# One layer of a two-layer DiT block: ctx's feed-forward network in a pass of its own, lat's up projection by seven products

## The chip, the cores and the metric

The kernel runs on one core of a Trainium2 chip. The metric is device time in microseconds: the median of three runs is 3036.41 us (3034.74 to 3040.76). Besides these there is one execution under the hardware profiler, and every row below is from it.

## The reference, cut to what matters

Two token streams go through two layers: lat, 1024 tokens, and ctx, 256 tokens, both of width 1024, all in float32. In layer 1 ctx only feeds lat's mixers; its own output is not needed there, so its feed-forward network (FFN) runs in layer 0 alone.

```python
def conv_ffn(h, w_up, conv_w, conv_b, w_down):
    u = dwconv(h @ w_up, conv_w, FFN_CONV // 2) + conv_b      # w_up 1024 x 5632, 3 taps along the tokens
    gate, val = jnp.split(u, 2, axis=-1)                      # D_FF = 2816 columns each
    return (jax.nn.silu(gate) * val) @ w_down                 # 2816 x 1024

for layer in range(DEPTH):                                    # DEPTH = 2
    mod = sc @ ada_w[layer] + ada_b[layer]                    # conditioning: 6 x 1024 numbers per stream
    mod_c = scc @ ada_w[layer] + ada_b[layer]
    ...
    y_l, y_c = token_mixer(h_l, h_c, w_in[layer], w_out[layer], ...)
    x = x + g1[:, None, :] * y_l
    x = x + g2[:, None, :] * conv_ffn(modulate(x, norm_ffn_g[layer], sh2, sc2), ffn_w_up[layer], ...)
    if want_ctx:                                              # layer 0 only
        h_ctx = h_ctx + g1c * y_c
        h_ctx = h_ctx + g2c * conv_ffn(modulate(h_ctx, norm_ffn_g[layer], sh2c, sc2c), ffn_w_up[layer], ...)
return rmsnorm(x, final_norm_g)
```

## The kernel before, in words

Activations lie transposed: 128 channels on the partitions, tokens along the free axis, so lat is 8 tiles of 128x1024 and ctx 8 tiles of 128x256. A float32 product is made of three passes of TensorE over operands cut in two parts: ACT casts the raw tile to the high part (L315), DVE subtracts it to get the low part (L316), and the passes are high by high, high by low, low by high (`mm3`, L341). A weight of 1024x128 is loaded as 512 KB into a raw tile (`load_w`, L325). The raw tiles come from rings "wr" and "wd" of one buffer each, the cut parts from rings "wh" and "wl" of two each. So a raw tile is loaded again only when its subtraction is done. PSUM holds two tiles of 1024 columns ("a") and four of 512 ("b").

A scheduler writes one queue per engine in advance. An engine works off its queue in that order; DMAs are issued by SP (weights) and POOL (activations), in order as well.

Each layer has these stages: the mixers (projections of lat and ctx, a gated scan, window attention, a linear recurrence); `project_out` (L1145 ff), in two parts of 512 lat tokens; the norm; the up projection; the down projection `lat_down`. The stages that the change touches are:

- **Layer 0's FFN** (`ffn_up`, about 790 to 1491 us of the span). For each of 22 column tiles f and for gate and value it loads one 512 KB tile of W_up. With that it makes 48 products of 512 columns for lat (tile `pu`) and 24 of 256 columns for ctx (`puc`). The convolution is one ACT operation and two on DVE (L1277 to L1279). For every two f, ctx's down products (`pd`, 48 of 256 columns) are made and added to the residual `xc` on DVE (L1257). A row block of W_down (`dr`, 512 KB) is loaded and cut for that, on ACT and DVE.
- **Layer 1's up projection** (`ffn_up7`, 2317 to 2783 us) has lat only. It cuts the 2x2 block product into seven products of sums of blocks (Strassen's scheme), tiles `ux` and `uz` (L1445): for each f 7 x 12 = 84 products of 512 columns for gate and value together, where the plain form has 96. The sums of activations are made in `sums7` (L1473) after the norm `norm7`, the sums of weights on DVE, beside the products.
- **Lat's down projection** (`lat_down`, tiles `px` and `py`, L1661): seven stages of six operand pairs each, in both layers. Its activations come back from DRAM (`park`); in layer 0 those of even f stay partly in SBUF.
- **The conditioning** (`ada_gen`): one step loads 512 KB of ada_w (`aw`, L190) and makes 4 float32 products of 256 columns (`ada`, L199; 8 records in the trace). A generator has 16 such steps. Those of layer 1's second and third part (32 steps) lie in layer 0: 28 in its FFN, 4 in its attention.
- **The final norm** (`fin`, L1681 to L1692): eight rows of 128 tokens, each transposed on TensorE, squared on ACT, scaled on DVE and stored. The last four come after the last product.

The rows name two more operations: L916, in attention, is the only elementwise work on POOL; L1409 and L1410 are the convolution in layer 1.

Of the kernel before, what the change touches and what calls it, by code (L numbers as in the profile page):

```python
# [18 lines left out]
P = 128  # L19
# [68 lines left out]
def tile_dit(ctx: ExitStack, tc: tile.TileContext, x, c, ctxt, c_ctx, ada_w, ada_b, norm_mix_g, norm_ffn_g,  # L88
# [371 lines left out]
    def ada_tile():  # L460
        aring[1] += 1
        return wtile(aring[0][aring[1] % len(aring[0])], "aw", F32, 1)

    adas += [ada_gen(l_, t_, ada_tile) for l_, t_ in ((0, 1), (0, 2), (1, 0), (1, 1), (1, 2))]
# [85 lines left out]
    def mixers(l, hl, hc, steps):  # L550
# [339 lines left out]

        lrus = [lru(p) for p in range(2)]
# [173 lines left out]
        def att_step(s_):  # L1065
# [17 lines left out]
            if l == 0 and s_ % 2 and s_ < 4 * len(grp) - 40:  # L1083
                ada_step()
# [38 lines left out]
        if l == 0:  # L1123
            ada_fin(0, 1)
# [19 lines left out]
    def project_out(l, y, xl, xc):  # L1144
# [18 lines left out]
        for part in range(2):  # L1163
            for m in range(KT):
# [28 lines left out]
    def ffn_up(l, h, hc_, xc, bt, pre_):  # L1193


        WU, WD = ffn_w_up[l], ffn_w_down[l]
        u_, odd, even, grp, cq = {}, {}, [], [], []
        jobs = [(0, h, T), (1, hc_, C)]

        def up_w(f, val):  # L1200
            return load_w((ALL, ALL, ALL, w_cols(WU, (f + NF * val) * P)))

        pre = {(0, v): up_w(0, v) for v in range(2)}
        yield "ready"

        def b_tile(a, j):
            if PAIRS[j][1] == 2:
                bt[a, 0, j] = two(L("b"))
            else:
                bt["odd", a] = two(L("b"))  # L1210
                bt[a, 0, j] = bt["odd", a][:, 0:1, :]

        def lat_act(f, g, u):
            fh, k = f % 2, f // 2
            j, i = k // 2, k % 2
            if fh == 0:
                if i == 0:
                    b_tile(fh, j)
                for b, o in ((0, bt[fh, 0, j][:, i, :]), (1, u[:, 512:1024])):
                    V.tensor_tensor(out=o, in0=g[:, b * 512:b * 512 + 512], in1=u[:, b * 512:b * 512 + 512], op=mult)  # L1220
            else:
                V.tensor_tensor(out=u, in0=g, in1=u, op=mult)
                G.dma_start(out=park[l][1, 0, j][:, i, :], in_=u[:, 0:512])
            if fh == 0:
                even.append(u)
                return
            e = even.pop()
            G.dma_start(out=park[l][1, 1, j][:, i, :], in_=u[:, 512:1024])
            V.tensor_tensor(out=e[:, 512:1024], in0=u[:, 512:1024], in1=e[:, 512:1024], op=sub)
            G.dma_start(out=park[l][0, 1, j][:, i, :], in_=e[:, 512:1024])  # L1230

        def ctx_act(f, a):

# [3 lines left out]
            split(dh, dl, dr)  # L1237
            ac = H2("ac", F32R)
            ah, al = ac[:, 0:C], ac[:, C:2 * C]
            split(ah, al, a)  # L1240
            grp.append((dh, dl, ah, al))
            if f % 2:
                g_ = list(grp)
                grp.clear()
                cq.extend((g_, m) for m in range(0, KT, 2))

        def ctx_down(g_, m):
            pd = pb1("pd")
            for i, (dh, dl, ah, al) in enumerate(g_):
                for m_ in range(2):  # L1250
                    c_ = slice((m + m_) * P, (m + m_ + 1) * P)
                    for pi in range(3):
                        PE.matmul(out=pd[:, m_ * C:(m_ + 1) * C], lhsT=(dl if pi == 2 else dh)[:, c_],
                                  rhs=al if pi == 1 else ah, start=(i == 0 and m_ == 0 and pi == 0),
                                  stop=(i == 1 and pi == 2), skip_group_check=True)
            for m_ in range(2):
                V.scalar_tensor_tensor(out=xc[m + m_], in0=pd[:, m_ * C:(m_ + 1) * C], scalar=mod[l][:, 40 + m + m_, 1:2],  # L1257
                                       in1=xc[m + m_], op0=mult, op1=add)

        def up(f, val):  # L1260
            col = f + NF * val
            wh, wl = pre.pop((f, val)) if (f, val) in pre else up_w(f, val)

            def cw(j):
                return rows[f"fcw{l}{j}"][:, col:col + 1]

            ada_load()
            if (f, val) == (NF - 1, 1):
                pre_()
            for s_, hh, n in jobs:  # L1270
                pu = pb1("puc")[:, 0:C] if s_ else ps("pu")
                for b in ((BC,) if s_ else (B0, B1)):
                    mm3(pu[:, b], wh, wl, *cut(hh, b))
                u = H2("uc")[:, 0:C] if s_ else L("u")
                if not val:
                    u_[s_, f] = u
                S.activation(out=u, in_=pu, func=AF.Identity, scale=cw(1), bias=rows[f"fcb{l}"][:, col:col + 1])  # L1277
# [10 lines left out]
            if not val:  # L1288
                while cq:
                    ctx_down(*cq.pop(0))  # L1290
            ada_mm()

        for f in range(NF):
            up(f, 0)
            up(f, 1)
# [512 lines left out]
```

## Time and profile before

| what | value |
|---|---|
| median of three runs | 3036.41 us |
| the profiled execution, its own time | 3035.6 us |
| its span, first to last instruction | 3033.8 us |
| TensorE busy | 2877.1 us, 95% |
| VectorE (DVE) busy | 1902.6 us, 63% |
| ScalarE (ACT) busy | 1420.8 us, 47% |
| GpSimd (POOL) busy | 236.5 us, 8% |
| mean granted TensorE clock | 0.981 |
| moved by DMA | 335.75 MB, mean 111 GB/s |

The span is 1.8 us shorter than the execution's own time. Busy time of TensorE is counted as the union of its pipelined products; the number of products in a stretch says more than the busy share where the clock falls. Stages have different limits, so the shares of the whole span say little about a single stage.

### The profile page before, as it was taken

To read this page: it belongs to the slowest core of one execution; us is meant where nothing else is said; L and a number is where in the kernel's file an instruction comes from. 1 tells how busy PE (TensorE), PEld (TensorE's weight loads), DVE (VectorE), ACT (ScalarE), POOL (GpSimd) and SP (SyncE) were. 2 spreads that over 40 slices of the span, in tenths; PEclk is the share of its full clock that TensorE was granted. 3 is DMA by queue.
4 is the path that set the end of the run, shared out by engine and by line. 5 is a ranking of instruction groups with operands and counts; after the bars stand their busy time and mean duration, and the time that the engine had idled before them with its cause. 6 is when DMAs were issued, how large, how long until landed. Compare 5 with 4: busy or idle time off the path is not lost. (4 is left out here: it accounts for less than half of the span.)

```text
span 3033.8 us, 41821 instructions
## 1 busy us (share of the span) xinstructions
PE 2877.1 (95%) x16208; PEld 2273.7 (75%) x16208; DVE 1902.6 (63%) x3005; ACT 1420.8 (47%) x2445; POOL 236.5 (8%) x348
## 2 busy tenths in 40 slices
PE   6999898999999999999999899998998899999998
PEld 5867676558888888888878787676667688877776
DVE  5466555665644444444587756776757777776876
ACT  5366764663422222222334545784745555544333
POOL 2000002000000000000101000002010011112010
PEclk9999999999999999999999999999999899999999
DMA  7211246424322332222576200124043333336762
GB/s 296 70 60 53 66 128 187 121 90 126 98 91 95 101 101 77 77 66 74 186 253 186 94 29 22 36 63 108 11 162 99 77 98 94 95 94 205 261 190 90
DMA packets 286678, 335.75 MB, mean 111 GB/s; under 512 B 19180, under 2 KB 211856, under 8 KB 286480
## 3 DMA queue, kind: packets, MB, share of 16 engines
q1 hardware_dynamic: 242928, 231.29, 24.6%
q0 software_dynamic: 43376, 101.73, 11.2%
q8 instruction: 128, 2.10, 0.3%
q14 instruction: 70, 0.57, 0.1%
q10 hardware_dynamic: 176, 0.07, 0.0%
HBM read 276.65 MB, written 56.36 MB: 110 GB/s over the span
## 5 line engine op out<-in xcount | busy, mean ns | idle before, releaser
L1445 PE MATMUL ux<-t,sw 128*128 128x512 f32 x1320 | 319.9, 398 | 20.5 <-ACT t L315 10.8
L1445 PEld LDWEIGHTS ux<-t,sw 128*128 128x128 f32 x1320 | 248.2, 190 | 85.3 <-ACT t L315 13.4
L341 PE MATMUL pu<-hh,wh 128*128 128x512 f32 x704 | 278.9, 397 | 0.1
L341 PE MATMUL pu<-hh,wl 128*128 128x512 f32 x704 | 276.5, 393 | 0.0
L341 PE MATMUL pu<-hl,wh 128*128 128x512 f32 x704 | 275.4, 391 | 0.0
L1278 DVE SCALAR_TENSOR_TENSOR u<-pu,col_fcb,u 128x1023 f32<-128x1023 f32 x44 | 56.4, 1283 | 324.6 <-ACT u L1277 324.6
L315 ACT CAST wh<-wr 128x1024 fp32r<-128x1024 f32 x110 | 115.2, 1049 | 230.8 <-PE pc L341 66.6
L341 PE MATMUL pl<-hh,wh 128*128 128x512 f32 x512 | 211.3, 413 | 2.0 <-ACT wh L315 0.8
L341 PE MATMUL pl<-hh,wl 128*128 128x512 f32 x512 | 205.7, 402 | 1.1 <-DVE wl L316 1.1
L341 PE MATMUL pl<-hl,wh 128*128 128x512 f32 x512 | 205.4, 401 | 0.0
L1277 ACT ACTIVATE u<-pu,col_nf,col_fcw 128x1024 f32<-128x1024 f32 x44 | 53.0, 1206 | 318.9 <-PE pu L341 318.9
L316 DVE TENSOR_TENSOR wl<-wr,wh 128x1024 fp32r<-128x1024 f32 x110 | 136.0, 1236 | 69.4 <-ACT wh L315 62.3
L341 PEld LDWEIGHTS pu<-hh,wh 128*128 128x128 f32 x704 | 132.3, 188 | 38.8 <-issue 11.8
L315 ACT CAST ah<-raw 128x512 fp32r<-128x512 f32 x132 | 76.0, 618 | 182.0 <-PE px L1661 89.3
L341 PEld LDWEIGHTS pu<-hh,wl 128*128 128x128 f32 x704 | 132.3, 188 | 29.1 <-DVE uc L1278 0.6
L341 PEld LDWEIGHTS pu<-hl,wh 128*128 128x128 f32 x704 | 132.4, 188 | 28.0 <-issue 0.2
L1445 PE MATMUL uz<-t,sw 128*128 128x512 f32 x528 | 132.4, 398 | 0.7 <-DVE cv L1460 0.7
L341 PEld LDWEIGHTS pl<-hh,wh 128*128 128x128 f32 x512 | 96.4, 188 | 35.2 <-issue 14.0
L1445 PEld LDWEIGHTS uz<-t,sw 128*128 128x128 f32 x528 | 100.5, 191 | 24.4 <-DVE cv L1460 1.6
L1011 DVE TENSOR_REDUCE st<-sc 128x1 f32<-128x641 f32 (+2 forms) x144 | 106.8, 745 | 17.8 <-ACT sc L1010 16.2
L341 PEld LDWEIGHTS pl<-hh,wl 128*128 128x128 f32 x512 | 96.6, 189 | 26.4 <-issue 5.1
L1014 ACT ACTIVATE pb<-sc,st 128x641 f32<-128x641 f32 (+2 forms) x144 | 106.3, 739 | 20.4 <-DVE st L1011 17.4
(464 smaller groups left out, 7352.6 us busy)
## 6 DMA issues: line engine op xcount, KB each, us to landing
raw<-in_ffn_w_down_dram SPq DMA_DIRECT2D x220, 256.0 KB
aw<-in_ada_w_dram SPq DMA_DIRECT2D x96, 512.0 KB
wr<-in_ffn_w_up_dram SPq DMA_DIRECT2D x44, 512.0 KB
b<-act POOLq DMA_DIRECT2D x35, 512.0 KB, 8.9
wr<-in_w_in_dram SPq DMA_DIRECT2D x34, 512.0 KB
act<-u POOLq DMA_DIRECT2D x66, 256.0 KB, 3.6
wr<-in_w_out_dram SPq DMA_DIRECT2D x128, 128.0 KB
dr<-in_ffn_w_down_dram SPq DMA_DIRECT2D x22, 512.0 KB
```

What stands on the lines that cost most here:

```text
L315: S.copy(out=hi, in_=raw)
L316: eng.tensor_tensor(out=lo, in0=raw, in1=hi.bitcast(F32), op=sub)
L341: PE.matmul(out=o, lhsT=wl[k] if pi == 2 else wh[k], rhs=hl[k] if pi == 1 else hh[k], start=(k == 0 and pi == 0), stop=(k == nk - 1 and pi ...
L1011: V.tensor_reduce(out=st[:, 0, c_], in_=sc[:, s0:769], axis=mybir.AxisListType.X, op=ALU.min)
L1014: S.activation(out=pb, in_=sc[:, s0:769], func=AF.Exp, bias=st[:, 0, c_], scale=-1.0, accum_out=st[:, 1, c_])
L1277: S.activation(out=u, in_=pu, func=AF.Identity, scale=cw(1), bias=rows[f"fcb{l}"][:, col:col + 1])
L1278: V.scalar_tensor_tensor(out=u[:, 1:n], in0=pu[:, 0:n - 1], scalar=cw(0), in1=u[:, 1:n], op0=mult, op1=add)
L1445: PE.matmul(out=out, lhsT=(al if pi == 2 else ah)[:, k * P:(k + 1) * P], rhs=rhs[k][1 if pi == 1 else 0], start=(i in (1, 2, 7) and k == 0 ...
```

## The change

In layer 0, `ffn_up` goes. In its place stand `ffn_ctx`, a pass over the 22 column tiles for ctx alone, and then `ffn_up7` for lat, as in layer 1. W_up of layer 0 is therefore loaded twice. In `ffn_ctx`, gate's raw weight uses the ring "wr" and value's the ring "wd"; the low part of the down weight is made on POOL; all 8 x 256 columns of ctx's output are summed over all f in the two large PSUM tiles and added to the residual once, at the end. Lat's norm of the upper half of the tokens and the sums of `sums7` are steps that are dealt out over the pass, two to a column tile at first, then one. `project_out` makes ctx's part in its first part instead of the second, and ctx's norm lies in the second part.

The 32 conditioning steps are now taken in layer 1's projections and attention, where their weight tile is again on the rings. Layer 0's norm steps at the end of `lat_down` are grouped. The last four rows of the final norm are cut: transposing, squaring and scaling by the weight for channels 512 to 1023 is done within the last stage, and only channels 0 to 511 come after it, with one reciprocal root for the four rows.

```diff
-    adas += [ada_gen(l_, t_, ada_tile) for l_, t_ in ((0, 1), (0, 2), (1, 0), (1, 1), (1, 2))]
+    adas += [ada_gen(l_, t_, ada_tile) for l_, t_ in ((0, 1), (0, 2), (1, 0))]
...
+        if l:
+            adas.extend(ada_gen(1, t_, ada_tile) for t_ in (1, 2))
...
-            if l == 0 and s_ % 2 and s_ < 4 * len(grp) - 40:
+            if s_ % 2 and s_ < 4 * len(grp) - (1 - l) * 40:
                 ada_step()
...
-                if part == 1 and xc is not None:
+                if part == 0 and xc is not None:
...
-    def ffn_up(l, h, hc_, xc, bt, pre_):
+    def ffn_ctx(l, hc_, xc):
...
+        po = [ps("pd") for _ in range(2)]
+        pd = [po[m // 4][:, m % 4 * C:(m % 4 + 1) * C] for m in range(KT)]
...
+            return load_w((ALL, ALL, ALL, w_cols(WU, (f + NF * val) * P)), ring=("wr", "wd")[val])
...
             dr = L("dr")
             nc.sync.dma_start(out=dr, in_=WD[f * P:(f + 1) * P, :])
             dh, dl = L("dh", F32R), L("dl", F32R)
-            split(dh, dl, dr)
+            split(dh, dl, dr, G)
+            return dh, dl
...
+        for f in range(NF):
+            ada_load()
+            u_ = []
+            for val in range(2):
+                col = f + NF * val
+                wh, wl = up_w(f, val)
+                if val == 0:
+                    dw = down_w(f)
...
+                pu = pb1("puc")[:, 0:C]
+                mm3(pu, wh, wl, *cut(hc_, BC))
...
+            if due:
+                down(*due.pop())
+            V.tensor_tensor(out=u_[0], in0=u_[0], in1=u_[1], op=mult)
             ac = H2("ac", F32R)
             ah, al = ac[:, 0:C], ac[:, C:2 * C]
+            split(ah, al, u_[0])
+            due.append((f, *dw, ah, al))
+            ada_mm()
+            yield
+        down(*due.pop())
+        for m in range(KT):
+            V.scalar_tensor_tensor(out=xc[m], in0=pd[m], scalar=mod[l][:, 40 + m, 1:2], in1=xc[m], op0=mult, op1=add)
...
+        fa, up_ = [lambda r=r: fin(r, xa) for r in range(4)], [lambda i=i: upper(i) for i in range(4)]
+        return [all_of(*fa[0:2]), all_of(*fa[2:4], up_[0]), all_of(*up_[1:4])], lower
...
-        f_ = ffn_up(l, h2, h2c, xc, bt, lambda: next(d_)) if want else ffn_up7(l, xl, tb, lambda: next(d_))
-        next(f_)
-        run(steps0)
+        f_ = ffn_up7(l, xl, tb, lambda: next(d_))
+        n1 = norm7(xl, 1, l, xmid[l], tb)
         if want:
...
+            run(stepsc)
+            todo, n1 = steps0 + n1[0:1], n1[1:]
+            todo += sums7(xl, tb, n1)
+            aring[0] = None
+            for i_, _ in enumerate(ffn_ctx(l, h2c, xc)):
+                run(todo, 1 + (i_ < 6))
+                if i_ == NF - 1:
+                    next(f_)
+            aring[0] = ["wd"]
+            next(f_)
+            run(todo)
```

Two places show what moves. The first is SP's queue at the start of layer 0's FFN. Before, `wr_7283` and `wr_7289` are gate and value of f = 0, `wr_7630` and `wr_7726` those of f = 1, then f = 2; `aw` is conditioning; `dr_7617` and `dr_7822` are the down weights of f = 0 and f = 1.

```order
L325 DMA wr_7283<-in_ffn_w_up_dram 128x8x128
L190 DMA aw_7439<-in_ada_w_dram 128x1024
L325 DMA wr_7289<-in_ffn_w_up_dram 128x8x128
L325 DMA wr_7630<-in_ffn_w_up_dram 128x8x128
L190 DMA aw_7529<-in_ada_w_dram 128x1024
L190 DMA aw_7636<-in_ada_w_dram 128x1024
L190 DMA aw_7732<-in_ada_w_dram 128x1024
L1235 DMA dr_7617<-in_ffn_w_down_dram 128x1024
L325 DMA wr_7726<-in_ffn_w_up_dram 128x8x128
L325 DMA wr_7835<-in_ffn_w_up_dram 128x8x128
L325 DMA wr_7991<-in_ffn_w_up_dram 128x8x128
L1235 DMA dr_7822<-in_ffn_w_down_dram 128x1024
```

The same place on SP in the changed kernel, from the down weight of f = 0 on. `wr_7405` and `wr_7447` are gate and value of f = 1, `wr_7524` and `wr_7566` of f = 2, `wr_7667` and `wr_7709` of f = 3, `wr_7780` and `wr_7822` of f = 4; `dr_7411`, `dr_7530` and `dr_7673` are the down weights of f = 1, 2 and 3.

```order
L1207 DMA dr_7316<-in_ffn_w_down_dram 128x1024
L325 DMA wr_7405<-in_ffn_w_up_dram 128x8x128
L325 DMA wr_7447<-in_ffn_w_up_dram 128x8x128
L325 DMA wr_7524<-in_ffn_w_up_dram 128x8x128
L325 DMA wr_7566<-in_ffn_w_up_dram 128x8x128
L325 DMA wr_7667<-in_ffn_w_up_dram 128x8x128
L325 DMA wr_7709<-in_ffn_w_up_dram 128x8x128
L1207 DMA dr_7411<-in_ffn_w_down_dram 128x1024
L325 DMA wr_7780<-in_ffn_w_up_dram 128x8x128
L325 DMA wr_7822<-in_ffn_w_up_dram 128x8x128
L1207 DMA dr_7530<-in_ffn_w_down_dram 128x1024
L1207 DMA dr_7673<-in_ffn_w_down_dram 128x1024
```

The down weight of f = 1 now stands behind the up weights of f = 3, and that of f = 2 behind those of f = 4.

The second place is TensorE's queue where it sums the squares of the upper half of lat's tokens (`pm`). Before, that is between the last products of `project_out` and the first of lat's up projection:

```order
L1160 MATMUL yoc_7253<-ych_6167,wh_7211 128x256
L1160 MATMUL yoc_7253<-ycl_6168,wh_7211 128x256
L1160 MATMUL yoc_7253<-ych_6167,wl_7212 128x256
L270 MATMUL pm_7299<-sq_7300,cft_66 128x512
L341 MATMUL pu_7441<-hh0_6241,wh_7285 128x512
L341 MATMUL pu_7441<-hl0_6249,wh_7285 128x512
L341 MATMUL pu_7441<-hh0_6241,wl_7286 128x512
```

In the changed kernel it is inside ctx's pass. Here `pd_7309` is the running sum of ctx's output, `ac_7626` with `dh_7532` and `dl_7533` the operands of f = 2, and `puc_7679` gate's product of f = 3:

```order
L1216 MATMUL pd_7309<-ac_7626,dh_7532 128x256 x2
L1216 MATMUL pd_7309<-ac_7626,dl_7533 128x256
L270 MATMUL pm_7629<-sq_7630,cft_66 128x512
L341 MATMUL puc_7679<-ch_6216,wh_7669 128x256
L341 MATMUL puc_7679<-cl_6218,wh_7669 128x256
L341 MATMUL puc_7679<-ch_6216,wl_7670 128x256
```

The down products of f = 1 and f = 2 and `pm_7629` all stand ahead of the up products of f = 3.

## Rows read from the trace of the kernel before

**Rows 1.** The page's first part: busy us, share of the span, instructions

```profile
PE 2877.1 (95%) x16208; PEld 2273.7 (75%) x16208; DVE 1902.6 (63%) x3005; ACT 1420.8 (47%) x2445; POOL 236.5 (8%) x348
```

**Rows 2.** Windows by stage, columns in the first line

```profile
core 0: us, PE busy (x) PEld busy (x) DVE busy (x) ACT busy (x) POOL busy (x), PEclk, DMA share, GB/s
790.00:850.00 60.00, 57.64 (x287) 45.23 (x287) 41.43 (x67) 30.53 (x49) 0.00 (x0) 0.97 0.27 86
850.00:1450.00 600.00, 600.00 (x3421) 511.15 (x3420) 271.29 (x371) 156.30 (x192) 16.13 (x30) 1.00 0.27 86
1450.00:1620.00 170.00, 162.75 (x762) 133.24 (x761) 128.96 (x166) 62.77 (x85) 26.11 (x41) 1.00 0.66 219
1730.00:2050.00 320.00, 311.95 (x2044) 246.84 (x2044) 210.61 (x359) 203.88 (x333) 8.12 (x9) 0.99 0.12 38
2310.00:2400.00 90.00, 73.00 (x293) 54.99 (x292) 71.37 (x105) 50.55 (x80) 6.13 (x7) 0.85 0.25 62
2400.00:2640.00 240.00, 240.00 (x1047) 195.39 (x1046) 179.51 (x237) 119.29 (x173) 30.68 (x39) 1.00 0.39 98
2640.00:2780.00 140.00, 135.28 (x583) 108.14 (x583) 101.99 (x134) 67.53 (x98) 21.11 (x29) 1.00 0.42 108
2780.00:2920.00 140.00, 129.41 (x545) 103.77 (x544) 112.61 (x140) 55.53 (x73) 22.29 (x34) 0.98 0.80 258
```

**Rows 3.** Chain of waits, 2560 to 2720: start, us, what

```profile
2572.98 11.03 PE ux L1445 x48
```

**Rows 4.** Operations by line, 790 to 1490: busy us, mean ns, idle before

```profile
L316 DVE TENSOR_TENSOR wl<-wr,wh 128x1024 fp32r<-128x1024 f32 x43 | 52.5, 1221 | 0.5 <-ACT wh L315 0.5
...
L315 ACT CAST wh<-wr 128x1024 fp32r<-128x1024 f32 x43 | 45.2, 1050 | 60.7 <-PE puc L341 59.0 <-DMA wr<-in_ffn_w_up_dram 1.7
...
L1278 DVE SCALAR_TENSOR_TENSOR uc<-puc,col_fcb,uc 128x255 f32<-128x255 f32 x44 | 21.0, 477 | 0.0
L199 PE MATMUL ada<-aw,cl 128*32 128x256 f32 x224 | 19.2, 397 | 1.1 <-DMA aw<-in_ada_w_dram 1.1
...
L1220 DVE TENSOR_TENSOR b<-u 128x512 f32<-128x512 f32 x11 | 7.5, 685 | 0.5 <-ACT u L1281 0.5
```

**Rows 5.** Windows of tile puc, 850 to 1450

```profile
850.00:1450.00 600.00, 111.89 (x912) 111.17 (x912) 36.30 (x76) 21.21 (x38) 1.00 0.27 86
```

**Rows 6.** Windows of tile pd, 850 to 1450

```profile
850.00:1450.00 600.00, 59.98 (x480) 58.89 (x480) 34.42 (x80) 1.00 0.27 86
```

**Rows 7.** Chain of waits, whole span: loads of 512 KB in layer 1

```profile
2367.48 3.77 DMA uv<-in_ffn_w_up_dram
...
2672.42 7.14 DMA uv<-in_ffn_w_up_dram
...
2753.57 5.58 DMA uv<-in_ffn_w_up_dram
```

**Rows 8.** Line L916 on POOL: ns min/median/max, first and last start

```profile
L916 POOL TENSOR_TENSOR rc<-ra,cst x20: 1261/1328/2343, 422.6 to 2087.3; 128x512 f32<-128x512 f32 x20
```

**Rows 9.** Windows of 10 us in layer 1's start, columns as in rows 2

```profile
2350.00:2360.00 10.00, 7.18 (x15) 4.12 (x15) 9.90 (x17) 4.79 (x9) 0.00 (x0) 0.50 0.00 0
...
2380.00:2390.00 10.00, 10.00 (x45) 8.21 (x44) 7.25 (x10) 5.57 (x8) 0.59 (x1) 1.00 0.25 79
```

**Rows 10.** Chain of waits, the end: start, us, what

```profile
3009.49 0.45 PE fo L1681 x4
...
3014.13 0.66 DVE xb L1613
...
3022.98 1.41 DVE ot L1692 x2
...
3025.89 1.41 DVE ot L1692 x2
...
3029.56 0.66 DVEq L1803
```

**Rows 11.** DMA queues, 820 to 1450: packets, MB, share of 16 engines

```profile
q1 hardware_dynamic: 49840, 47.19, 24.2%
```

More of the change, by code (lines that the diff above doesn't have):

```diff
@@ L1191, in two, with down_w @@
         return t_.rearrange("p (a t) -> p a t", a=2)
[L1193 removed]
+    def ffn_ctx(l, hc_, xc):
         WU, WD = ffn_w_up[l], ffn_w_down[l]
[L1197 to L1198 removed]
+        po = [ps("pd") for _ in range(2)]
+        pd = [po[m // 4][:, m % 4 * C:(m % 4 + 1) * C] for m in range(KT)]
         def up_w(f, val):
[L1201 to L1232, printed above, removed]
+            return load_w((ALL, ALL, ALL, w_cols(WU, (f + NF * val) * P)), ring=("wr", "wd")[val])
+        def down_w(f):
             dr = L("dr")
@@ L1236, in ctx_act, with down @@
             dh, dl = L("dh", F32R), L("dl", F32R)
-            split(dh, dl, dr)
+            split(dh, dl, dr, G)
+            return dh, dl
+        def down(f, dh, dl, ah, al):
+            for m in range(KT):
+                c_ = slice(m * P, (m + 1) * P)
+                for pi in range(3):
+                    PE.matmul(out=pd[m], lhsT=(dl if pi == 2 else dh)[:, c_], rhs=al if pi == 1 else ah,
+                              start=(f == 0 and m % 2 == 0 and pi == 0), stop=(f == NF - 1 and pi == 2), skip_group_check=True)
@@ L1238, in ctx_act @@
             ac = H2("ac", F32R)
             ah, al = ac[:, 0:C], ac[:, C:2 * C]
[L1240 to L1277, printed above, removed]
-                V.scalar_tensor_tensor(out=u[:, 1:n], in0=pu[:, 0:n - 1], scalar=cw(0), in1=u[:, 1:n], op0=mult, op1=add)
-                V.scalar_tensor_tensor(out=u[:, 0:n - 1], in0=pu[:, 1:n], scalar=cw(2), in1=u[:, 0:n - 1], op0=mult, op1=add)
-                if not val:
-                    S.activation(out=u, in_=u, func=AF.Silu)
-                elif s_:
-                    g = u_.pop((1, f))
-                    V.tensor_tensor(out=g, in0=g, in1=u, op=mult)
-                    ctx_act(f, g)
-                else:
-                    lat_act(f, u_.pop((0, f)), u)
-            if not val:
-                while cq:
-                    ctx_down(*cq.pop(0))
-            ada_mm()
@@ L1758, in after @@
                     hn.append((new_h(L, "h"), new_hc()))
-                    fins.extend(norm_block([xa(k, 0) for k in range(KT)], *hn[0][0], B0, 1, 0, 0))
+                    st_ = norm_block([xa(k, 0) for k in range(KT)], *hn[0][0], B0, 1, 0, 0)
+                    fins.extend(lambda a=a: run(st_, a) for a in (1, 3, 3, 2))
                 if si == 6:
```

127 lines of the change are left out of this document (82 added, 45 removed).

## The prediction

> **What bounds the kernel now.** I read the page's busy shares first, and the reader is to see there that TensorE is busy for 95% of the span [rows 1], so that a change pays mainly by products that go, or by gaps that open or close. Next I read the windows by stage [rows 2], since stages have different limits. In 850 to 1450, layer 0's FFN, TensorE is busy for 600.00 of 600 us; in 2400 to 2640, layer 1's seven products, for 240.00 of 240. Both steady states are bound by TensorE alone, with DVE at 45% and 75%. The gaps lie at the seams: 2.4 us in 790 to 850, 17 us of busy time in 2310 to 2400 (where the clock is 0.85 besides), 4.7 and 10.6 us in 2640 to 2780 and 2780 to 2920. Third, the chain of waits in layer 1's up projection [rows 3] gives the price of a product of 512 columns: 48 in 11.03 us. With the 1047 that 2400 to 2640 counts in its 240 us, 0.2292 us, I take 0.2295 each. Fourth, the operations by line in layer 0's FFN [rows 4] give what surrounds the products.
>
> **The change part by part.**
>
> *Lat's up projection in layer 0.* 22 column tiles times 12 products fewer, 264 x 0.2295 = 60.6 us less. That the seven products, with all their sums of weights and activations on DVE, hold TensorE full is what 2400 to 2640 shows, so this term is nearly sure.
>
> *Ctx's products.* 1056 up and 528 down products of 256 columns stay. In the steady stretch they cost 111.89/912 = 0.123 and 59.98/480 = 0.125 us [rows 5, 6]; they cancel. What does not cancel is cover. Before, each weight tile fed 48 lat products (11 us) as well; now one column tile f gives TensorE 48 x 0.123 + 24 x 0.125 = 8.9 us, and within these three loads of 512 KB, three casts and three subtractions must pass. DVE has per f two subtractions of 1.22, four convolution steps of 0.48 and two of about 0.42 for ctx, 5.2 us, and of lat's norm and sums by the code some 50 operations of 128x512 at 0.69 over 22 f, 1.6 us: 6.8 us, under 8.9. ACT has less. A raw ring turns in landing + 1.05 (cast) + 1.22 (subtraction) + about 0.4 for queueing. A landing is 3.77 us where a load is alone and 7.14 or 5.58 where it meets activation stores [rows 7], so a turn is 6.4 to 9.8 us; with 5.6 it is 8.3, just under 8.9. I therefore count the steady part at TensorE's pace, and nothing for the ring.
>
> *The start of the pass.* On SP the down weight of f = 1 stands behind f = 3's raw weights, which wait for the ring, two turns after f = 0's subtraction. Then follow the landing, a cast and the subtraction on POOL. POOL's only such row is 128x512 in 1.26 to 2.34 us, mostly 1.33 [rows 8]; I take twice 1.26, 2.5 us, for 128x1024, with 4.7 as the upper end. Sum: 2 x 8.3 + 5.6 + 1.05 + 2.5 + 0.4 = 26.2 us. TensorE has until then f = 0, 1, 2 and f = 0's down products, 7 x 24 x 0.123 = 20.7 us, and some 1.5 us head start of the first weights: it waits 4 us. The down weight of f = 2 comes one turn later, 8.3 us, and TensorE has only 24 products (3.0 us) between, as the order puts f = 3 behind: another 5.3 us. The sum of squares `pm` behind it, with its eight squares behind a down weight's cast on ACT, I put at 2. Together 11 to 12 us; nothing if the loads run at 3.8, 25 if they run at 7.1 and POOL at 4.7. The clock may follow: in layer 1's start TensorE, busy for 7.18 of 10 us, was granted 0.50 and issued 15 products instead of 45 [rows 9]. Here it is busy for some 60% of 25 us. I add 3 us, from 0 to 13. In all 15 us.
>
> *The rule that speaks against POOL's subtraction.* POOL's own row has a spread: one 128x512 took 1.26 us, another 2.34, with no cause shown [rows 8]. The Trainium skill (SBUF — State Buffer, "Who interferes with whom") says that a DVE instruction with two inputs in SBUF contends with a GpSimd instruction that reads SBUF, and that the one which comes second is fully blocked until the other ends. By that rule POOL's 2.5 us would fall on DVE's weight subtractions, once per f, and a raw ring's turn would go from 8.3 to as much as 10.8 us. No run here shows it yet; the spread of POOL's row agrees with it, since it is almost a doubling. The time it would give is the third rival's.
>
> *The end of the pass.* The last convolution and split (about 1 us), then 24 products, and the first product of lat wants a PSUM tile that holds four of ctx's sums: 4 x 0.48 on DVE [rows 4]. With the remaining casts of the sums, which are covered by the first products, 4 us, from 0.5 to 9. What the lat FFN of layer 1 loses at its own start, 17 us of busy time, is not added, since its norm and sums are made beside ctx's products.
>
> *Lat's down projection of layer 0.* It now follows seven products, as in layer 1, with the convolution of the last tile at the end and all activations read back. Layer 1 shows the loss in 2640 to 2920: 280 us less (583 + 545) x 0.2295 = 21.1 us [rows 2]. Layer 0 lost 7.3 of 170 us in 1450 to 1620. So +14, from 0 to 18.
>
> *The start of the FFN.* The 2.4 us gap of 790 to 850 goes: ctx's norm is made beside `project_out`.
>
> *Conditioning.* 28 steps, 224 records, 19.2 us [rows 4], leave layer 0, where TensorE is full, and enter layer 1's projections, where it is busy for 311.95 of 320 us [rows 2]. So they cost there what they saved. The four of the attention cost nothing either way, since it has gaps. Their weight tile takes a turn of the same raw ring as the projections' weights; I put 2 us, from -3 (they fill gaps) to +6.
>
> *The end.* After the last product four `xb` operations end at 3014.8, then each row of the final norm takes 2.9 us, to 3029.56, and the last store ends 4.2 us later [rows 10]. After the change remain four squares, one root and four scalings of 0.7 us (1.41 for two), about 8 us from 3014.8, but four stores of 512 KB then leave together. At the weight queue's rate, 47.19 MB in 24.2% of 630 us [rows 11], about 309 GB/s, they need 6.8 us, 5 more than one. 16 transposes go into the last stage (four in 0.45 us, 1.8 us in all). Net -4, from -8 to +1.
>
> *The sum.* -60.6 + 15 + 4 + 14 - 2.4 - 4 + 2 = -32.0 us against the profiled execution's 3035.6, hence 3003.6. The median of the runs is 0.8 above that execution, hence **3004**.
>
> **The rivals.**
>
> *All hidden.* The loads run near 3.8 us, as they do alone; the pass loses 5 instead of 19, the down projection 6 instead of 14, and the end gives 6. Then -60.6 + 5 + 6 - 2.4 - 6 + 1 = -57, **2979**. For it: three loads per f take 1.57 MB, at 309 GB/s 5.1 of 8.9 us, so the queue has room. Against: three loads in 8.9 us seldom run alone, and the last tile's tail stands in layer 1's rows.
>
> *The slow start spreads.* If TensorE stays at the lower clock for some 20 us after the first gaps, and each of the first f waits a little, the pass loses 40 instead of 19: -11, **3025**. For it: 2350 to 2360 at 0.50 [rows 9]. Against: a lower clock lets the loads catch up.
>
> *The other side: ctx's pass is bound by its raw rings.* If each f takes a ring's turn instead of TensorE's 8.9 us, every 0.1 us of it costs 2.2 us. It decides from 8.9 + 32/22 = 10.35 us on. A landing of 7.14, POOL's subtraction in DVE's way for 1.8 us, cast, subtraction and queueing make 11.6: 22 x 2.7 = 59 us, of which the clock's share and the start's 15 are partly the same, so 45: +13 against before, **3049**. For it: the 7.14 row, one raw buffer per ring, lat's stores in the same time. Against: the two rings alternate, so that a load meets one other more often than two.
>
> *Seven products that aren't TensorE's in layer 0* would undo the first term. 240.00 of 240 in layer 1, with the same operations, leaves it 2 in 100.
>
> **How the numbers follow.** The forecast has 0.53, all hidden 0.20, the spreading start 0.15, the ring 0.10, the last 0.02. The forecast alone reaches from 2990 to 3016. The range takes in the first two rivals, 2976 to 3036, and leaves out most of the ring's and a little at the low end. A measurement of this kernel can tell about 0.2%, 6 us, from no change. Faster than 3030 are the forecast, the first rival and nearly all of the second: 0.86; within 0.2% is 0.04; slower 0.10.
>
> **What would show it.** In the profile after: `puc` and `pd` in a stretch of about 196 us plus the pass's stalls; TensorE full from about the eighth f on, at 8.9 us per f (the ring would show as a wait for `wh` or `wl` in every f, and a landing over 6 us); two gaps of 4 to 5 us before `pd` in the first 40 us, released by POOL or by the cast of the down weight; 1848 products `ux` and `uz` in layer 0 in about 424 us; in the following down projection the gaps of 2640 to 2920 again; layer 1's projections some 20 us longer. It is wrong if the pass takes over 230 us, if POOL's subtraction takes 4 us, or if the last stores end less than 2 us earlier after the last product than now.

## The result, and the profile after

The changed kernel takes 2987.38 us in the median of four runs (2983.74 to 2999.64) against 3035.57 before: ratio 0.985, 95% interval 0.982 to 0.988, 48 us less where 32 were forecast. It lies inside the stated range, 2976 to 3036, but 3 us under the 2990 to which the forecast alone reached. The profiled execution is the longest of the four (span 2997.9). A second profile, of run e1 below (2982.3), differs from it by 1 to 4 us in six stages and by much in none, so the length of a single stage is known to about 3 us.

The page's first part answers to [rows 1]. 264 products are gone from TensorE; DVE, ACT and POOL are busier:

```profile
PE 2824.4 (94%) x15944; PEld 2222.4 (74%) x15944; DVE 2065.2 (69%) x3199; ACT 1572.8 (52%) x2715; POOL 333.5 (11%) x417
```

Windows by stage of the profile after, columns as in [rows 2]. Ctx's pass is 783 to 1006, lat's seven products in layer 0 1006 to 1440, its down projection to 1666, layer 1's projections 1672 to 2046:

```profile
783.00:804.00 21.00, 20.08 (x168) 19.66 (x167) 14.66 (x22) 12.60 (x18) 1.90 (x2) 1.00 0.56 167
804.00:828.00 24.00, 15.26 (x70) 13.12 (x69) 15.65 (x21) 15.70 (x25) 7.51 (x3) 0.72 0.33 114
828.00:1006.00 178.00, 165.61 (x1356) 161.17 (x1354) 148.81 (x198) 99.62 (x153) 43.43 (x18) 0.99 0.51 158
1006.00:1440.00 434.00, 427.54 (x1850) 344.85 (x1851) 318.83 (x423) 215.65 (x318) 57.01 (x73) 1.00 0.39 100
1440.00:1666.00 226.00, 217.09 (x926) 173.71 (x924) 177.72 (x231) 93.75 (x131) 31.03 (x48) 0.99 0.64 207
1672.00:2046.00 374.00, 369.38 (x2438) 276.04 (x2438) 230.72 (x387) 219.31 (x358) 18.67 (x19) 0.99 0.31 91
```

The length of each stage in us, from the first start of its own products on TensorE to that of the next stage's; the first row is a time from the start of the span. e1 is the changed kernel again, e7 the kernel before with only the conditioning moved, e2 and e12 are variants of the changed kernel; all are told below.

| stage | before | after | e1 | e7 | e2 | e12 |
|---|---|---|---|---|---|---|
| start of `project_out`, layer 0 | 669.1 | 667.0 | 663.6 | 664.8 | 664.6 | 664.7 |
| `project_out` | 121.5 | 116.2 | 114.6 | 119.3 | 114.6 | 114.8 |
| ctx's pass | | 223.1 | 221.1 | | 204.3 | 197.6 |
| lat's up projection (before, e7: whole FFN) | 694.8 | 433.4 | 433.0 | 670.1 | 434.5 | 431.2 |
| down projection, to layer 1 | 235.2 | 231.9 | 232.1 | 237.7 | 232.7 | 229.5 |
| layer 1's projections | 356.7 | 374.6 | 373.2 | 373.6 | 373.3 | 374.4 |
| attention | 145.8 | 141.8 | 142.0 | 142.3 | 142.1 | 142.7 |
| `project_out` and up projection | 560.1 | 561.2 | 557.3 | 555.6 | 559.7 | 560.2 |
| last down projection | 229.5 | 233.5 | 230.3 | 229.9 | 232.7 | 235.6 |
| behind the last product | 21.1 | 15.2 | 15.1 | 21.1 | 15.7 | 15.4 |

What TensorE waits for in ctx's pass (us in total, times, longest), the five largest, after:

```profile
PE puc L341 <- DVE wl L316: 8.9, 10, 2.1
PE pd L1216 <- ACT ac L315: 3.7, 6, 0.9
PE pd L1216 <- POOL dl L316: 3.2, 2, 1.7
PE pm L270 <- DVE sq L268: 3.1, 1, 3.1
PE pd L1216 <- ACT dh L315: 2.4, 2, 2.2
```

And three groups of operations there (busy us, mean ns, idle before), after; the first answers to the weight subtraction of [rows 4], which took 1221 ns:

```profile
L316 DVE TENSOR_TENSOR wl<-wr,wh 128x1024 fp32r<-128x1024 f32 x43 | 62.5, 1453 | 21.5 <-ACT wh L315 21.3
L316 POOL TENSOR_TENSOR dl<-dr,dh 128x1024 fp32r<-128x1024 f32 x22 | 53.3, 2425 | 155.1 <-ACT dh L315 147.0 <-PE pd L1216 4.2 <-PE puc L341 3.9
L1243 DVE TENSOR_TENSOR uc<-uc 128x256 f32<-128x256 f32 x22 | 23.1, 1049 | 0.9 <-ACT uc L1240 0.3
```

POOL keeps its 2.4 us; DVE's operations with two inputs in SBUF grow. TensorE's largest wait, 8.9 us in all, is for the very operand (`wl`) that DVE makes late.

The end in the chain of waits, after (start, us, what), for [rows 10]: squares of channels 0 to 511 on ACT, then the root (left out here), and the last two of four scalings on DVE, which end at 2992.0:

```profile
2985.21 2.43 ACT ot L1679 x8
...
2990.70 1.32 DVE ot L1686 x2
```

### The profile page after: what moved, and what is told of

Read it like the earlier page. It is cut to its first block, busy times and chain, and to the rows that moved or that the text cites. A ratio compares the mean times of both kernels' runs of the same rounds, so it can differ in the third digit from the quotient of the medians.

```text
span 2997.9 us, 42218 instructions
## 1 busy us (share of the span) xinstructions
PE 2824.4 (94%) x15944; PEld 2222.4 (74%) x15944; DVE 2065.2 (69%) x3199; ACT 1572.8 (52%) x2715; POOL 333.5 (11%) x417
## 5 line engine op out<-in xcount | busy, mean ns | idle before, releaser
L1400 PE MATMUL ux<-t,sw 128*128 128x512 f32 x2640 | 632.5, 396 | 26.7 <-ACT t L315 10.8
L1400 PEld LDWEIGHTS ux<-t,sw 128*128 128x128 f32 x2640 | 493.3, 189 | 153.1 <-ACT cv L1412 14.4
L1400 PE MATMUL uz<-t,sw 128*128 128x512 f32 x1056 | 260.8, 395 | 1.1 <-DVE cv L1415 1.1
L1400 PEld LDWEIGHTS uz<-t,sw 128*128 128x128 f32 x1056 | 199.5, 189 | 47.0 <-DVE cv L1415 2.7
L341 PE MATMUL pl<-hl,wh 128*128 128x512 f32 x512 | 204.3, 399 | 0.0
L315 ACT CAST sw<-s 128x512 fp32r<-128x512 f32 x176 | 109.3, 621 | 95.0 <-DVE s L1309 75.3
L316 DVE TENSOR_TENSOR sw<-s,sw 128x512 fp32r<-128x512 f32 x176 | 121.4, 691 | 47.5 <-ACT sw L315 41.0
L1015 DVE TENSOR_REDUCE st<-sc 128x1 f32<-128x641 f32 (+2 forms) x144 | 106.4, 745 | 16.9 <-ACT sc L1014 15.2
L341 PEld LDWEIGHTS pl<-hl,wh 128*128 128x128 f32 x512 | 96.2, 188 | 23.7 <-issue 6.7
L316 DVE TENSOR_TENSOR al<-raw,ah 128x512 fp32r<-128x512 f32 x132 | 86.0, 687 | 38.4 <-ACT ah L315 31.5
L341 PE MATMUL puc<-ch,wl 128*128 128x256 f32 x352 | 100.0, 284 | 8.9 <-DVE wl L316 8.9
L665 ACT COPY qz<-Q 64x512 f32<-64x512 f32 (+1 forms) x140 | 86.0, 614 | 37.0 <-DVE Q L705 31.0
```

The source lines that it names most:

```text
L315: S.copy(out=hi, in_=raw)
L316: eng.tensor_tensor(out=lo, in0=raw, in1=hi.bitcast(F32), op=sub)
L341: PE.matmul(out=o, lhsT=wl[k] if pi == 2 else wh[k], rhs=hl[k] if pi == 1 else hh[k], start=(k == 0 and pi == 0), stop=(k == nk - 1 and pi ...
L665: S.copy(out=o_, in_=view[hsl(hd)])
L1015: V.tensor_reduce(out=st[:, 0, c_], in_=sc[:, s0:769], axis=mybir.AxisListType.X, op=ALU.min)
L1400: PE.matmul(out=out, lhsT=(al if pi == 2 else ah)[:, k * P:(k + 1) * P], rhs=rhs[k][1 if pi == 1 else 0], start=(i in (1, 2, 7) and k == 0 ...
```

## The experiments

Times are medians; each ratio is to the kernel before in the same session, with its 95% interval. The kernel before itself took 3034.73 us in the session of e1 to e4, 3035.78 in that of e5 to e8, 3034.09 in that of e9 and e10 and 3031.04 in that of e11 and e12, so runs of different sessions are compared by their ratios too. "Lost" below is the length of a stretch less 0.115 us for each product in it, the price that e2 shows (under "Why the prediction was right").

**e1, the changed kernel again.** 

> The changed kernel again, unaltered, for a second profile and for the spread of its times. Its profiled execution took 2999.6 us, three others 2983.7 to 2988.4, while the kernel before stays within 7 us. Theory A (chance in the pass): the 37 us that ctx's pass lost in that profile are partly chance (loads that meet, clock dips at 800 to 826 and 930 to 940), and the missing 12 us are there: a second profile of a faster execution shows a pass of 208 to 215 us instead of 223 and the other stages within 2 us. Theory B (chance elsewhere): the pass is again 221 to 225 us and the difference is in layer 1 or in the down projections.

2987.85 us, ratio 0.985 (0.984 to 0.987). The pass takes 221.1 us, and 224.7 in e8, which leaves it as it is: its gaps are no chance. The 15 us between the two profiles lie in pieces of up to 4 us along the whole program, half of them ahead of layer 1. Theory B is right about the pass, but names too few places for the rest.

**e2, the down weight's low part on DVE.** 

> Ctx's pass with the low part of the down weight made on DVE, not on POOL (one argument of one call). Theory P (shared port): in the profile after, DVE's operations with two inputs in SBUF took longer while POOL worked: the weight subtraction 1453 ns in the mean against 1221 before, the product of gate and value 1049 against 422; over the pass some 30 us of DVE time. Without POOL these go back to 1221 and 422, DVE gains 22 x 1.22 = 27 us of work and loses about 30 us of blocking: the pass gets 0 to 8 us shorter (waits of TensorE for wl go from 8.9 us to under 4). Theory Q (POOL unloads DVE, as the change intends): DVE is the neighbour that sets the weights' pace, 27 us more on it make the pass 5 to 20 us longer.

```diff
-            split(dh, dl, dr, G)
+            split(dh, dl, dr)
```

2975.12 us, ratio 0.981 (0.979 to 0.982): 12 to 13 us faster than the changed kernel; the pass takes 204.3 us, 17 to 19 less, and other stages of this profile are up to 2.4 us longer than e1's. The same lines of e2's pass:

```profile
L316 DVE TENSOR_TENSOR wl<-wr,wh 128x1024 fp32r<-128x1024 f32 x43 | 52.5, 1220 | 11.7 <-ACT wh L315 11.3
L316 DVE TENSOR_TENSOR dl<-dr,dh 128x1024 fp32r<-128x1024 f32 x21 | 25.6, 1221 | 11.3 <-ACT dh L315 11.3
L1243 DVE TENSOR_TENSOR uc<-uc 128x256 f32<-128x256 f32 x22 | 9.3, 421 | 0.7 <-ACT uc L1240 0.2
```

and its wait for `wl`:

```profile
PE puc L341 <- DVE wl L316: 1.6, 4, 1.1
```

DVE does 22 subtractions more, and the kernel is faster all the same: the blocking cost more. Theory P holds, with twice its upper price for the pass. The start of the pass still loses 11.4 us in 799 to 819 (16 before, in 804 to 828), and the rest of it 8.2 instead of 22: some 5 of the gain lie in the start, 13 behind it.

**e10, POOL's subtraction alone, in the kernel before.** 

> The kernel before with one part of the change alone: the low part of the down weight (22 times) on POOL instead of DVE. There each column tile gives TensorE 31 us, and DVE is busy 45%. Theory A (DVE's operations with two inputs in SBUF are held up by POOL here too, but nobody waits for them): L316 wl or the products of gate and value are longer in the mean by 100 to 400 ns, POOL's 22 take 2.4 us each, and the time is within 4 us of before. Theory B (POOL's subtraction costs time in itself, by its 2.4 us of latency on the way to the down products): 5 us or more slower.

```diff
-            split(dh, dl, dr)
+            split(dh, dl, dr, G)
```

3035.99 against 3034.09 us, ratio 1.001 (1.000 to 1.002). By line (ns min/median/max), before and then e10, an operation of 128x512 beside POOL:

```profile
L1229 DVE TENSOR_TENSOR u<-u x11: 678/681/683, 858.6 to 1486.4; 128x512 f32<-128x512 f32 x11
```

```profile
L1229 DVE TENSOR_TENSOR u<-u x11: 2485/2506/2515, 856.9 to 1487.9; 128x512 f32<-128x512 f32 x11
```

The same blocking, 1.8 us eleven times here and some 13 us more on L1220 and on `ac`, costs 2 us by the medians, 1 to 7 by the interval, where TensorE has 31 us of work per column tile. The names of the delayed lines were others than I expected (`wl` is untouched), and POOL's own subtraction is longer too, 2.91 us in the median and up to 3.32. Theory A holds. The order of the two can be read from e10's timeline (start, us):

```profile
855.37 1.22 DVE L1222 TENSOR_TENSOR u<-u 128x1024 f32<-128x1024 f32 x1
855.68 3.18 POOL L316 TENSOR_TENSOR dl<-dr,dh 128x1024 fp32r<-128x1024 f32 x1 [20.61 <-ACT dh L315]
856.90 2.51 DVE L1229 TENSOR_TENSOR u<-u 128x512 f32<-128x512 f32 x1
```

POOL starts while DVE's L1222 runs and takes 0.8 us more than its 2.4; L1229 starts while POOL runs and ends 0.55 us after it, about its own 0.68. In both cases the one that starts second waits.

**e3, down weights two tiles ahead.** 

> Ctx's pass with each down weight's load and cut requested two column tiles ahead, so that on the queue of loads those of f = 1 and f = 2 stand ahead of most up weights of f = 1 and f = 2, not behind those of f = 3 and f = 4. Theory A (the queue's order makes the slow start): the gaps before the down products of f = 1 and f = 2 (the stretch 804 to 828 gives TensorE 81 products, 9.3 us of work, in 24 us) shrink from about 15 to 5 us, and the clock dip with them: 6 to 12 us faster than the changed kernel. Theory B (the sum of squares sets it): pm stands on TensorE ahead of f = 3 in this order too, so the wait for it stays and grows by what the others lose: 0 to 3 us faster.

```diff
+        dws = [down_w(0), down_w(1)]
...
-                    dw = down_w(f)
+                    dw = dws.pop(0)
+                    if f + 2 < NF:
+                        dws.append(down_w(f + 2))
```

2999.65 us, ratio 0.989 (0.987 to 0.991): 12 us slower than the changed kernel. The pass takes 225.9 us, 3 to 5 more; the rest of the 12 is spread over other stages. The gap is as large and stands later: 18.6 us are lost in the 40 below. Windows of 20 us, e3:

```profile
803.00:823.00 20.00, 11.53 (x77) 0.83 0.53 176
823.00:843.00 20.00, 16.85 (x109) 0.83 0.20 58
```

(columns: PE busy (x), clock, DMA share, GB/s.) The waits for `dl` and `dh` are gone from its list; waits for `wl` (12.7 us) and `ac` (8.5) take their place. SP's order alone did not make the gap. Neither theory had foreseen a loss.

**e5, the norm of the upper half later (on e2).** 

> e2 (low part of the down weight on DVE) with lat's norm and sums dealt out the other way round: one step per column tile for the first five, then two, in place of two for the first six, then one. The sum of squares of the upper half and its burst of eight squares on ACT (4.3 us) and seven additions on DVE (5.5 us) come about three column tiles later, when the rings run. Theory A (the burst, with pm on TensorE ahead of the next up products, makes the slow start): the gap at 800 to 818 (30 us of the pass give TensorE 149 products, 17 us of work) shrinks, the clock stays at 1.00: pass 194 to 200 us instead of 204.3, time 5 to 10 us under e2's 2975. Theory B (the late loads of the down weights and the filling of the rings make it): the gap stays where it is and a second one comes with the burst: pass 203 to 212 us.

```diff
-                run(todo, 1 + (i_ < 6))
+                run(todo, 1 + (i_ > 4))
```

2969.17 us, ratio 0.978 (0.977 to 0.980): 6 us under e2, as theory A has it. But the pass, 202.2 us, is only 2.1 shorter than e2's, and 5.4 of the profile's 7.6 lie in the last down projection, which the edit does not touch. What it shows is the place: the start runs through without waiting for down weights, and the gap has gone with the squares and `pm` to 822 to 837, where 8.9 us are lost. Windows of e2 and of e5, columns as for e3:

```profile
799.00:819.00 20.00, 15.31 (x75) 0.66 0.44 156
```

```profile
822.00:837.00 15.00, 10.32 (x53) 0.77 0.42 135
```

One scheduler writes all queues, so the edit changes SP's order as well. In e2 three down weights leave together, in e5 one at a time between up weights (SP's timeline, e2 and then e5; start, us):

```profile
803.51 1.52 SPq L1207 DMA_DIRECT2D dr<-in_ffn_w_down_dram  x3
```

```profile
802.97 0.57 SPq L1207 DMA_DIRECT2D dr<-in_ffn_w_down_dram  x1
```

By itself e5 doesn't tell the burst from the order of loads; together with e3 and e6 it does.

**e6, e5 with down weights one tile ahead.** 

> e5 with each down weight's load and cut requested one column tile ahead. e3 showed that this alone, with POOL's subtraction and the early burst, made the kernel 12 us slower. Theory A (in e3 the burst was the limit and the earlier down weights only pushed up weights back): with the burst late, the early down weights fill the last waits: 2 to 6 us faster than e5. Theory B (each 512 KB ahead of an up weight delays the up weight, and that is what TensorE waits for first): 3 to 10 us slower than e5.

```diff
+        dws = [down_w(0)]
...
-                    dw = down_w(f)
+                    dw = dws.pop(0)
+                    if f + 1 < NF:
+                        dws.append(down_w(f + 1))
```

2975.36 us, ratio 0.980 (0.979 to 0.981): 6 us slower than e5. That is theory B's time, but its reason does not show: TensorE waits 3.0 us for `wl` where e5 has 2.5. The pass takes 205.6 us, 3.4 more, and its last column tile bears that, with a wait of 4.8 us for `ac` where e5 has 1.9. In 822 to 837 it loses 8.0 us, e5 8.9. So with the burst early (e3) and with the burst late (e6), loading the down weights sooner hardly changes the gap, and its place follows the burst.

**e9, the squares in five steps (on e5), and e11, e12.** 

> e5 with the sum of squares of the upper half cut into five steps: two squares on ACT and two additions on DVE per step, the product pm with the root in the fifth. In e5's profile the gap moved with the burst: in 822 to 837, where squares and pm now stand, TensorE makes 55 products in 15 us instead of 135, some 9 us lost with the clock at 0.66 to 0.91. Theory A (the burst is the gap): the gap goes, the pass takes 192 to 197 us instead of 202.2, time 5 to 9 us under e5's 2969. Theory B (the gap is the chain squares, additions, pm, root that the next norm steps wait for, however it is cut): the pass is 200 to 205 us, time within 3 us of e5.

```diff
+        return [lambda k0=k0: part(k0) for k0 in range(0, KT, 2)] + [end]
...
-            todo, n1 = steps0 + n1[0:1], n1[1:]
+            todo, n1 = steps0 + n1[0:5], n1[5:]
```

Each `part` is two squares and their additions, `end` is `pm` and the root. 2975.15 us, ratio 0.981 (0.980 to 0.982): 6 us slower than e5 by the medians, 8 by the ratios; the pass takes 204.9 us. That is theory B's pass, though not its time, and not theory A. The gap is smaller, 6.9 us lost in 832 to 847, but it remains, with 3.7 us for `ac`, the split activation of a column tile whose up products have only just ended:

```profile
841.96 0.80 PE L1240 MATMUL pd<-ac,dh 128*128 128x256 f32 x2 [3.69 <-ACT ac L339]
```

The 4.2 us that the next expectation names are another wait for `ac`, at 980, in the last column tile of the pass:

```profile
980.13 1.08 PE L1240 MATMUL pd<-ac,dh 128*128 128x256 f32 x3 [4.17 <-ACT ac L339]
```

From the last up product to lat's first the pass takes 12.3 us in e9 and 8.8 in e5, which is more than the two passes differ by. In TensorE's queue the down products of the newest column tile, and then `pm`, stand ahead of the next up products. Two runs took that on, e11 on e5 and e12 on e9, both with the down products two tiles later (what is left at the end of the pass is made there):

```diff
-            if due:
-                down(*due.pop())
+            if len(due) > 1:
+                down(*due.pop(0))
```

> e5 with the down products of a column tile made two tiles later instead of one. In e5 and e9 TensorE's queue has, just ahead of pm, the down products of the newest column tile right behind those of the one before, and waits there 2.8 and 4.2 us for ac, with the clock at 0.50 to 0.66 behind it. Theory A (that order is the gap): with operands that are long ready the wait for ac goes, the clock stays at 1.00, the pass takes 193 to 198 us instead of 202.2, time 4 to 9 us under e5's 2969. Theory B (the burst of squares holds up ACT and DVE, and with them the next weights): the wait moves to pm or to wl, the pass stays at 200 us or more, time within 3 us of e5.

> e9 (squares in five steps) with the down products two column tiles later. Theory A as for e11: the pass takes 192 to 197 us instead of e9's 204.9, time 6 to 12 us under e9's 2975. Theory B: if the burst were the gap, e9 would have closed it already; it did not, so under B some other wait of about 4 us remains in 837 to 847, the pass is 200 to 205 us and the time within 4 us of e9.

e11 2971.44 us (0.980, 0.979 to 0.982), 2 us over e5 by the medians and 7 by the ratios, pass 206.6 us: the wait moved to `pm` (2.5 us) and the weights, theory B; 6.7 us are lost in 822 to 837, and the end of the pass, with two tiles' down products in it, takes 14.6 us. e12 2968.04 us (0.979, 0.978 to 0.981), pass 197.6 us: 7 us under e9 by the medians, 5 by the ratios, with intervals that overlap. That is nearer to theory A, but the wait that theory B named is there too, in 837 to 847, with 4.1 us lost. The gap in e9, e11 and e12 (columns as for e3):

```profile
832.00:847.00 15.00, 11.07 (x70) 0.78 0.57 176
822.00:837.00 15.00, 11.21 (x72) 0.89 0.24 88
837.00:847.00 10.00, 8.41 (x51) 0.83 0.53 160
```

In the gap itself the loss goes from 11.4 us (e2) to 8.9 (e5), 6.9 (e9), 6.7 (e11) and 4.1 (e12). So the burst of squares on ACT and DVE, and a queue in which the newest tile's down products and `pm` come first, both have a part in it, by one profile of each run, in which the order of the loads shifts a little too; the later down products with the early burst were not tried. Over the whole pass, e9 and e11 lose at its end what they gain in the gap. e12 and e5 are equally fast within their intervals, the fastest of all versions, some 17 to 21 us under the changed kernel.

**e7, the conditioning moved, alone, in the kernel before.** 

> The kernel before with one part of the change alone: the 32 conditioning steps of layer 1 taken in layer 1's projections and attention. Theory A (the forecast): TensorE pays 19.2 us in either place, so within 5 us of the kernel before. Theory B (the traces of after and e4: layer 1's attention 142.0 instead of 145.8, layer 0's attention and output projection shorter by some 5 to 9): layer 0's FFN 19 us shorter, layer 1's projections 17 us longer, layer 1's attention 3 to 4 us shorter, layer 0's attention 3 to 5 us shorter: 7 to 12 us faster than before.

```diff
-    adas += [ada_gen(l_, t_, ada_tile) for l_, t_ in ((0, 1), (0, 2), (1, 0), (1, 1), (1, 2))]
+    adas += [ada_gen(l_, t_, ada_tile) for l_, t_ in ((0, 1), (0, 2), (1, 0))]
...
+        if l:
+            adas.extend(ada_gen(1, t_, ada_tile) for t_ in (1, 2))
```

(with the two conditions in the attention and at the end, as in the change.) 3017.22 us, ratio 0.994 (0.993 to 0.995): 14 to 22 us faster by this part alone, more than theory B. The FFN is 24.7 us shorter, layer 1's projections only 16.9 longer. All 32 steps lie in these projections, none in layer 1's attention, though the source allows it: 256 records, the first at 1749.7, the last at 2062.5, and the attention's first product of scores at 2065.5. They are busy for 22.3 us there, while TensorE's idle time in the stage falls from 9.5 to 3.6 us: the gaps took in 5.9. Layer 0's attention has 26 steps instead of 30, and what follows it starts 4.3 us earlier; layer 1's attention is 3.5 us shorter with no step in it in either kernel, for a reason that stays open. TensorE's timeline before shows one step in the FFN:

```profile
1018.22 0.28 PE L341 MATMUL puc<-ch,wl 128*128 128x256 f32 x1
1018.42 0.64 PE L199 MATMUL ada<-aw,cl 128*32 128x256 f32 x8
1018.99 0.50 PE L341 MATMUL pu<-hh,wh 128*128 128x512 f32 x1
1019.33 0.39 PE L341 MATMUL pu<-hl,wh 128*128 128x512 f32 x1
1019.56 0.39 PE L341 MATMUL pu<-hh,wl 128*128 128x512 f32 x1
```

From the start of `puc` to that of `pu` are 0.77 us where products without a step between them follow in 0.12, and the next product follows after 0.34 instead of 0.23: 0.76 us a step against 0.69 of busy time. For 28 steps that is 21 of the 24.7; the rest is not settled.

**e4, the conditioning in ctx's pass.** 

> The 32 conditioning steps stay in layer 0: 4 in its attention, 28 in ctx's pass (two per column tile for the first eight, then one), with their weights in tiles of their own; the rest as in the changed kernel. Theory A (they cost TensorE the same anywhere, as forecast): layer 1's projections get 17 to 19 us shorter, ctx's pass 15 to 19 us longer, layer 0's attention 2 to 3 us longer, layer 1's attention 4 us longer: within 6 us of the changed kernel. Theory B (they fill the gaps of ctx's pass, where TensorE waits 37 us anyway): the pass grows by 5 to 10 us only: 6 to 14 us faster. Theory C (14 MB more of loads in the pass delay the raw weights): the pass grows by 25 us or more: 5 to 20 us slower.

3000.38 us, ratio 0.989 (0.987 to 0.990), 13 us slower than the changed kernel. The pass takes 236.0 us, 13 to 15 more, layer 1's projections 355.5, 18 to 19 less, its attention 144.6, 3 more. Theory A's pieces came, but with layer 0's attention and `project_out` (start 668.8, 119.6 long; e1: 663.6 and 114.6) they don't cancel. The 14 MB that the steps load are in the pass too, and the run does not tell their part from that of the steps.

**e8, the old end.** 

> The changed kernel with the final norm as it was before: all of the last four rows after the last product. Theory A (the forecast, net 4 us, as the new stores leave together): 2 to 6 us slower than the changed kernel's 2987; the last down projection 1 to 3 us shorter, the stretch after the last product 21 us instead of 15. Theory B (the profile after shows 15.2 us behind the last product instead of 21.1, and the last down projection hardly longer): 5 to 7 us slower.

2996.13 us, ratio 0.987 (0.986 to 0.988): 8 us slower than the changed kernel by the medians of e1 and e8, 5 by their ratios; 21.4 us behind the last product, 6 more. The last down projection takes 228.1 us, 2 to 5 less, which is theory A's sign. Over all profiles it takes 231.3 in the mean of the ten with the new end and 228.5 in the four with the old one (before, e7, e8, e10). So the profiles give a net of some 3 us, the times 5 to 8, and the run does not settle which theory holds.

## Why the prediction was right, point by point

The direction and the size came, but by terms that were wrong on both sides, and that the sum came within 16 us is in part luck. In number the measured 2987 is nearer to the first rival, *all hidden* at 2979, but that rival's reason did not come: it had the pass lose 5 us, and it lost 39 to 41.

- **Seven products, -60.6:** right. 1848 of them take 433.4 us, 424.1 at 0.2295.
- **The seams, +14:** about 10. The up projection loses 9.3 us, which were counted to the down projection; that one is 3.3 us shorter than before, and before it held 32 of ctx's down products, some 4 us.
- **Ctx's pass, 196 + 19 = 215:** it took 221 to 223. A product costs less than in [rows 5, 6]: in e2, 895 to 955 holds 522 in 60.00 us, 0.115 each. The busy time of one tile counts the whole of each group's last product, which lasts 0.28 us while the next one starts 0.12 after it. So 1584 need 182 us, and the pass lost 39 to 41, not 19.
- **The start of the pass, +15:** it lost as much: 24 - 70 x 0.115 = 16 us in 804 to 828, with the granted clock at 0.72 in the mean. It changes there between its two levels, 1.00 (2.4 GHz) and 0.50 (1.2 GHz): after 804 to 806, in which TensorE was busy for 0.47 of 2 us, it falls, and 810 to 812, full at 0.50, holds 11 products where 800 to 802, full at 1.00, holds 20. The two waits before `pd` that the prediction named came, 3.2 us for POOL and 2.4 for the cast, and `pm` with 3.1; but SP's order, to which I put them down, does not set the loss: with the loads ahead it is as large (e3), and the gap goes where the norm's burst goes (e5, e6). Some 5 us of the start are POOL's subtraction (e2), some 7 go when the burst is moved and spread and TensorE's own order changed (e2 to e12), and the last 4 stay open. TensorE in windows of 2 us of the start, after, columns as for e3:

```profile
800.00:802.00 2.00, 2.00 (x20) 1.00 0.58 161
804.00:806.00 2.00, 0.47 (x5) 1.00 0.44 133
808.00:810.00 2.00, 0.61 (x3) 0.50 0.61 148
810.00:812.00 2.00, 2.00 (x11) 0.50 1.07 385
```

- **The steady part of the pass, "at TensorE's pace, and nothing for the ring",** is the first step that failed: 178 - 1356 x 0.115 = 22 us, of which about 2 are the end of the pass, where 4 were counted. In e2 the same part loses 8.2: some 13 were POOL's subtraction in DVE's way.
- **POOL's subtraction in DVE's way** was put into a rival at 0.10, with 1.8 us in each of 22 column tiles. A 128x512 operation grew from 0.68 to 2.51 us beside POOL (e10), and the changed kernel's pass paid 17 to 19 us in all (e2), under 1 us per column tile. So the price was less than the rival's, and the result did not go to the other side. The Trainium skill (SBUF — State Buffer, "Who interferes with whom") says that a DVE instruction with two SBUF inputs contends with a GpSimd instruction that reads SBUF, and calls the shared ports an exclusive lock. The trace agrees: in e10 either one waits for the other.
- **Conditioning, "they cost there what they saved", +2:** the step that failed by most: -19 in e7, some -13 by e4. Its busy time was right, the cancelling was not. A step between two streams of products cost 0.76 us where it is busy for 0.69, 2 us in all; layer 1's projections had 5.9 us of gaps for the steps; and layer 0's attention, where the prediction let four steps cost nothing, ended 4.3 us earlier without them. The section on the change puts some of the steps into layer 1's attention, but all 32 were made before it. Of e7's 19 us some 7 (the rest of the FFN's and layer 1's attention) have no cause shown.
- **The start, -2.4:** `project_out` with what follows is 5 to 7 us shorter; about 2 of that is conditioning's (e7).
- **The end, -4:** 6 us less behind the last product; in all 5 to 8 by e8's times, some 3 by the profiles. From the end of the last DVE operation to the end of the span it is now 5.9 us. Before it was 3.6, not the 4.2 that the prediction reads from [rows 10], since the last row's scaling runs on past 3029.56, to 3030.22; the four stores cost 2.3 us more than one, where 5 were assumed. The last row's scaling, before (start, us):

```profile
3028.81 1.41 DVE L1692 SCALAR_TENSOR_TENSOR ot<-fo,xst,fing 128x512 f32<-128x512 f32 x2
```

The pass came out 6 to 8 us worse, the seams some 4 better, conditioning 15 to 21 better, the start 1 to 2 better, the end about as forecast or up to 4 better: -32 became -48, as closely as stages known to 3 us add up.

## What to carry to other kernels

A neighbour's cover is part of a stage's price: what costs 2 us beside 31 us of products per column tile (e10) costs 12 to 13 us where 8 are left (e2). So before work goes to GpSimd, look for two-input operations of VectorE at the same time and for who waits for them. Small products in a full stream of TensorE are priced by the distance between their neighbours, not by their busy time, and belong where it has gaps; look in the trace where they really ran. When a gap moves with every remedy, ask for the second wait behind it before the next try, and look where in the stretch each wait stands: a list of waits has no places.

## What was not expected of the hardware

The last down projection, with the same instructions on TensorE, DVE and ACT in e2, e5, e9, e11 and e12, took 225.4 to 235.6 us in their profiles, a spread of 10 us, more than any of the last edits was worth. Layer 1's attention was 1 to 4 us shorter in each kernel that makes the conditioning steps in the projections ahead of it (141.8 to 143.3) than in before, e4 and e10, which make them in layer 0 (144.5 to 145.8); no step falls in it, and why it is shorter is open.
